# The MLP's last block: two pairs of K tiles as seven products in its first down pair and one in its second, rows turned by GpSimd's queue

## The chip, the cores and the metric

The kernel runs on one core of a Trainium2 chip. The metric is the device time of one execution in microseconds (us), as the median of several runs. A core has five engines with a queue of instructions each: TensorE (PE, matrix products into the accumulators in PSUM), VectorE (DVE, elementwise work and 32x32 transposes), ScalarE (ACT, elementwise work and functions), GpSimd (POOL, here mostly an issuer of DMAs) and SyncE (SP, here only an issuer of DMAs). Each engine runs its own queue strictly in order, and waits for the others by semaphores. So an instruction that waits also holds up everything behind it in its queue.

## The reference

The reference is a decoder trunk of two layers on 256 positions of width 2048: layer 0 with dilated attention, layer 1 with a sparse attention. Behind its attention each layer has an MLP and a gated embedding ("ple"):

```python
hn = rmsnorm(h, mlp_norm_g[i])
h = h + jnp.square(jax.nn.relu(hn @ mlp_w1[i])) @ mlp_w2[i]
gate = jax.nn.sigmoid(rmsnorm(h, ple_norm_g[i]) @ ple_w_gate[i])
h = h + (p[i] @ ple_w_proj[i]) * gate
```

All arrays are float32. `mlp_w1[i]` is 2048 x 8192 and `mlp_w2[i]` 8192 x 2048. The change touches only the second product of the MLP, in both layers, and the way its result gets back into the residual stream `h`.

## The kernel before

**Precision.** A float32 product is computed as three products of rounded parts (`terms`, line 464): each operand is split into a high part (type fp32r) and the rest. For weights, ACT makes `whi` from the loaded tile `raw` (line 249), DVE makes `wlo` as the difference (line 257). A weight chunk is a tile of 128 x 1024: two K tiles of 128 rows by 512 columns.

**The MLP.** It is cut into four blocks `b` of 2048 hidden features (`NFB` is 4), each with four quarters `q` of 512 columns. For every block the first product ("up") makes the hidden quarters, which are turned so that features lie on the partitions (`hid[b]`), and the second product ("down") makes four rows of sums, `q` = 0 to 3, each 128 x 2 x 512: 256 tokens by 512 columns. The rows of blocks 0 to 2 are added up in DRAM (`y[q]`, line 849). The last block, `b` = 3, adds what is in `y[q]`, turns the row (`turned`, line 695: a transpose in blocks by DVE into a tile `z`, one DMA out to DRAM, four DMAs back into a tile `w`), adds it to the residual stream (`add_turned`, line 718) and begins the next norm (`in_pairs`, line 725: ACT makes high part and square of four feature tiles, DVE their low parts and the sum of squares `acc`).

**Pairs and seven products.** `pair_major` (line 467) computes two quarters at once, with four accumulator banks for them. An item of its order is either one chunk of one quarter (`q0` or `q1`: two K tiles, two halves of tokens, three terms: 12 matmuls), or a pair of K tiles for both quarters by seven block products in place of eight (Strassen's scheme in Winograd's form). Such a seven-product pair is four items, in the text called a, b, t and u, with 6, 3, 6 and 6 matmuls. The items a and b use loaded chunks, t and u use sums of these that DVE makes (`make_t`, line 537; `make_u`, lines 542 and 543). The forms of the hidden features that it multiplies (`hf`, lines 782 to 794) are made once in `up`. Four of its products go to banks of their own, which `seven_sums` (line 805) adds up behind the last seven-product pair.

**The last block.** Before the change the first down pair of the last block (`down_mixed(3, 0)`, rows 0 and 1) has one seven-product pair, K tile pair 1, in the order (0,0) (0,2) (0,3), a b t u, (1,0) (1,2) (1,3), then chunks 4 to 7 of both rows. Rows 2 and 3 are not made as a pair: `downs(3, 2)` and `downs(3, 3)` run plainly, one after the other, eight chunks of 12 matmuls each (`token_major`, line 575). Their evacuation, line 857, adds the accumulator to the sums so far, which two DMAs (`fetch`, line 843) have brought from `y[2]` and `y[3]`. Rows 0 and 1 are added to `y[q]` by an accumulating DMA into the row (line 897). All four rows of the last block are turned by SP's queue, the same that loads the weights. Rows 0, 2 and 3 use the tiles `z` and `w`, of which there is one each; row 1 uses two tiles of the ring of rows (`second`).

**What sets the order.** `Program.run` (line 127) goes through the items. At item n it issues, in this order: the loads up to item n + 7 as far as one of five buffers is free, the high part of item n + 4 with its sum by DVE (`make_t`, `make_u`) if it has one, the low part of item n + 3, then one step of every evacuation under way (each `yield` in the code is the end of one step), and then the matmuls of item n. Evacuations are thus counted in items, not in time: `turned` issues its transpose at one item, the DMA out at the next, the DMAs in two items later, and the row is added two items after that.

**Behind the MLP.** `ple` has two projections (`w_proj`, two items) that need only the embedding, then 16 items of two gate quarters, interleaved two and two by `taken_late` (line 650). Their chunk c reads the feature tiles 2c and 2c + 1, so row 2 is wanted from the ninth gate item on and row 3 from the thirteenth. Behind the ninth, `norm.factor` (line 322) puts two small matmuls on PE that read `acc`, the sum of squares over all 16 feature tiles.

Of the kernel before, what the change touches and what calls it, by code (L numbers as in the profile page):

```python
# [11 lines left out]
F32R = mybir.dt.float32r  # L12
# [3 lines left out]
P = 128  # L16
# [18 lines left out]
DMA_AHEAD = 7  # L35
SPLIT_AHEAD = 3
RAW_BUFS, HI_BUFS, LO_BUFS = 5, 6, 5
MIXED_DOWN = 1
MIXED = (2, 3, 5, 6)
REST = ((6, 8, 2, 3), (4, 4, 2, 3))  # L40

# [3 lines left out]
def mixed(b, q):  # L45

    return MIXED[:4 if b else 3]


def f32(ap):  # L50
    return ap.bitcast(F32)
# [116 lines left out]
def kernel(ctx: ExitStack, tc: tile.TileContext, a: dict, out: bass.AP):  # L168
# [549 lines left out]
    def add_turned(q, w):  # L718

        for n in range(2):  # L720
            xn = xp[2 * q + n].rearrange("p (f a r) -> p f a r", a=4, r=32)
            wn = w.rearrange("p a (f r) -> p f a r", r=32)[:, 4 * n:4 * n + 4]
            nc.vector.tensor_add(xn, wn, xn)

    def in_pairs(make, q):

        for n in (0, 2):
            gs = [make(4 * q + n + i) for i in range(2)]
            for g in gs:
                next(g)  # L730
            yield
            for g in gs:
                next(g, None)

    def mlp(layer, xg, norm, to, norm2, opening):
# [15 lines left out]
        def row():  # L751
            return row_tile()
# [9 lines left out]
        def up(b, q, t, late=0):  # L762
            rest = REST[b > 0][q]

            nc.scalar.activation(t, t, AF.Square)
            for _ in range(2 + late):
                yield
            w = yield from turned(t, second if b == 0 and q == 1 else other if q % 2 else new, nc.gpsimd)
            for _ in range(rest):
                yield  # L770
            w4 = w.rearrange("p a (i j r) -> p a (i j) r", j=2, r=32)
            h = cur["z"].tile([P, 2, 4, T], F32R, tag="h", name="h", bufs=4)
            h5 = h.rearrange("p c i (j a r) -> p c a (i j) r", j=2, r=32)
            nc.scalar.copy(h5[:, 0], w4)
            yield
            nc.vector.tensor_sub(h5[:, 1], w4, f32(h5[:, 0]))  # L776
            for i in range(4):
                hid[b][4 * q + i] = (h[:, 0, i], h[:, 1, i])
            if q != MIXED_DOWN // 2:
                return  # L780

            n = MIXED_DOWN % 2 * 4
            a11, a21, a12, a22 = (w4[:, :, n + i] for i in range(4))
            nc.vector.tensor_sub(a22, a21, a22)
            nc.vector.tensor_sub(a21, a11, a21)
            nc.vector.tensor_sub(a11, a11, a22)
            nc.vector.tensor_sub(a12, a12, a11)
            yield
            f = cur["z"].tile([P, 2, 2 * T], F32R, tag="hf", name="hf", bufs=1)
            f5 = f.rearrange("p c (i a r) -> p c a i r", i=4, r=32)  # L790
            nc.scalar.copy(f5[:, 0], w4[:, :, n:n + 4])
            yield
            nc.vector.tensor_sub(f5[:, 1], w4[:, :, n:n + 4], f32(f5[:, 0]))
            turned_forms[b][MIXED_DOWN] = f

        def up_plain(b, q, ps0, ps1, mm):

# [49 lines left out]
        def keep_sum(b, q, t):  # L847

            nc.gpsimd.dma_start(y[q], flat(t), **({"accum_op": ALU.add} if b else {}))

        def down(b, q, ps0, ps1, mm):
            t = row() if b < NFB - 1 else sums_so_far[q]
            for j, ps in enumerate((ps0, ps1)):
                if b < NFB - 1:
                    nc.scalar.copy(t[:, j], ps)
                else:
                    nc.vector.tensor_add(t[:, j], ps, t[:, j])
            yield
            if b < NFB - 1:
                keep_sum(b, q, t)  # L860
                return
            w = yield from turned(t, second if q == 1 else new)
            add_turned(q, w)
            yield
            yield from in_pairs(normed, q)

        def chunks(w, b, q):
            return lambda c: a[w][layer * 128 + (b * 4 + q) * 8 + c]

        def ups(b, q, hooks=None):  # L870
            token_major(chunks("w1", b, q), xg, lambda *ps: up_plain(b, q, *ps), hooks, whole=True)

        def downs(b, q):
            token_major(chunks("w2", b, q), hid[b], lambda *ps: down(b, q, *ps), whole=True)

        def all_forms(these):
            for c in these:
# [4 lines left out]
        def down_mixed(b, q):  # L882
            ts = []

            def sums(aux):
                yield from seven_sums(aux, ts)

            def done(i, ps):
                while not ts:
                    yield  # L890
                t = ts[i]
                nc.vector.tensor_add(t, ps, t)
                yield
                if b < NFB - 1:
                    keep_sum(b, q + i, t)
                    return
                nc.gpsimd.dma_start(flat(t), y[q + i], accum_op=ALU.add)
                for _ in range(3):
                    yield
                w = yield from turned(t, second if q + i == 1 else new)  # L900
                add_turned(q + i, w)
                yield
                yield from in_pairs(normed, q + i)

            m = MIXED_DOWN
            p = [c for c in range(KT // 2) if c != m]
            order = [(0, c) for c in p[:3]]
            order += [(m,)] + [(1, c) for c in p[:3]] if b else [(1, c) for c in p[:3]] + [(m,)]
            for n in (3, 5):
                order += [(i, c) for i in range(2) for c in p[n:n + 2]]  # L910
            pair_major(lambda i, c: a["w2"][layer * 128 + (b * 4 + q + i) * 8 + c], order, hid[b], turned_forms[b],
                       sums, done, {13: [lambda: all_forms(MIXED[3:])]} if (b, q) == (0, 0) else None, (3, 1, 0, 2))

        up_mixed(0, 2)
        for b in range(NFB):
            down_mixed(b, 0)
            if b < NFB - 1:
                up_mixed(b + 1, 0)
                down_mixed(b, 2)
                up_mixed(b + 1, 2)  # L920
        prog.op(lambda: fetch(2))
        prog.op(lambda: fetch(3))
        downs(NFB - 1, 2)
        downs(NFB - 1, 3)
        prog.op(lambda: close_pool("z"))
        prog.op(lambda: open_pool("j"))
        prog.op(lambda: open_pool("R", side="right"))
# [971 lines left out]
def _layout(i):  # L1899
    a = dict(_tables())  # L1900
    a["xT"] = _feature_major(i["x"][0])
    a["xTA"] = _feature_major(i["x"][0][_order()])
    a["pT"] = np.stack([_feature_major(i["p"][l, 0]) for l in range(2)])
    gains = [i["attn_norm_g"][0], i["attn_norm_g"][1], i["mlp_norm_g"][0], i["mlp_norm_g"][1],
             i["ple_norm_g"][0], i["ple_norm_g"][1], i["kv_norm_g"], i["final_norm_g"]]
    a["gains"] = np.stack([g.reshape(KT, P).T for g in gains], 1)
    a["xg0"] = np.concatenate([a["xTA"][:, :2 * T], a["gains"][:, G_ATTN]], 1)
    w = i["a_w_in"][0].reshape(D, 3, NGA, HA, DH)
    a["w_qk"] = _singles(w[:, :2].transpose(0, 3, 1, 2, 4).reshape(D, -1))
    v = w[:, 2]  # L1910
    a["w_v"] = _quads(np.concatenate([t.reshape(D, -1) for h in (0, 4) for t in
                                      (v[:, 0, h:h + 4], v[:, 1:, h:h + 4].transpose(0, 2, 1, 3))], 1))
    a["w_oA"] = _quads(i["a_w_out"][0])
    a["w1"] = np.concatenate([_mixed(_quads(i["mlp_w1"][l]), range(2, 16, 2), mixed) for l in range(2)])
    a["w2"] = np.concatenate([_mixed(np.concatenate([_quads(i["mlp_w2"][l, b * D:(b + 1) * D]) for b in range(NFB)]),
                                     range(0, 14, 2), lambda b, q: (MIXED_DOWN,)) for l in range(2)])
    a["w_gate"] = np.concatenate([_quads(i["ple_w_gate"][l]) for l in range(2)])
    a["g_last"] = np.broadcast_to(i["final_norm_g"][D - 512:], (P, 512))
    a["w_proj"] = np.concatenate([_quads(i["ple_w_proj"][l]) for l in range(2)])
    a["w_kv"] = _quads(i["w_kv_shared"])  # L1920
    qg = i["b_w_qg"][0]
    a["w_q"] = _singles(qg[:, :HB * DH])
    gate = np.concatenate([qg[:, HB * DH:], np.zeros((D, 64 - 3 * HB), np.float32)], 1)
    a["w_g"] = gate.reshape(KT, P, 64).transpose(1, 0, 2).reshape(P, CH)
    a["w_oB"] = _quads(i["b_w_out"][0])
    a["w_c1"] = np.concatenate([i[n].reshape(8, 4, P, 256).transpose(0, 2, 1, 3).reshape(8, P, CH)
                                for n in ("cmp_w1_k", "cmp_w1_v")])
    for n in ("k", "v"):
        a["w2_" + n] = i["cmp_w2_" + n].reshape(2, P, DH).transpose(1, 0, 2)
        a["pe_" + n] = i["cmp_pe_" + n].T  # L1930
    return {n: np.ascontiguousarray(v) for n, v in a.items()}
# [20 lines left out]
```

## Time and profile before

| what | us |
|---|---|
| median of 3 runs (2421.16 to 2421.32) | 2421.16 |
| the profiled execution, its own time | 2421.02 |
| its span, first to last instruction | 2419.1 |
| PE busy, L499 (all pairs) and L595 (all plain quarters) among it | 2409.0 |
| DVE busy | 1988.5 |
| ACT busy | 1420.2 |
| the last block's first down pair in layer 1, from 2221.75 | 42.84 |
| its two plain quarters, from 2264.59 to 2308.11 | 43.52 |

The busy times are sums over the whole span. The granted clock of TensorE was 0.999. Line numbers in the profile are those of the code above. An operation is told as out<-in: `wlo<-raw,whi` is a low part, `ts<-raw` the sum t, `raw<-ts,raw` and `raw<-raw` the sum u, `z<-y` the transpose of a row, `dU<-z` and `w<-dU` the DMAs of its turn, `x<-w,x` its addition to the residual stream. In a timeline the columns are start, busy time, engine, line, operation, count, and in brackets the idle time before with what ended it. Instructions on one engine overlap a little, so that the next start is what one costs, not its busy time.

### The profile page before, as it was taken

The page shows a single profiled execution, that of the slowest core. Times are in us where ns is not written, and L with a number is a line of the kernel's source. Part 1 is how long each engine was busy: PE and PEld are TensorE (multiplying, and loading weights), DVE is VectorE, ACT ScalarE, POOL GpSimd, SP SyncE. Part 2 cuts the span into 40 slices and gives each one's busy share as a digit, 9 for nine tenths or more (in the row PEclk, how much of TensorE's full clock was granted, in tenths as well). Part 3 has the DMA queues.
Part 4 walks back from the last instruction along what each step waited for, and adds up shares of the span by engine and source line. Part 5 has one row for each costly group of instructions (what it writes and reads, how often), then busy time and mean ns, then how long its engine had stood idle before and what let it go on. Part 6 is the DMA issues. An engine that isn't in the chain of part 4 may idle for free.

```text
span 2419.1 us, 33339 instructions
## 1 busy us (share of the span) xinstructions
PE 2409.0 (100%) x11643; PEld 2029.3 (84%) x11643; DVE 1988.5 (82%) x2944; ACT 1420.2 (59%) x2069; POOL 122.0 (5%) x214
## 2 busy tenths in 40 slices
PE   9999999999999999999999999999999999999998
PEld 8888888888888888888888889988888888888887
DVE  7867687688898898896777989867899898889776
ACT  6544444566555655564564788756655565556456
POOL 0000000000001000100000000000100100100000
PEclk9999999999999999999999999999999999999999
DMA  8667666777778777879786854477867877777974
GB/s 284 200 220 213 199 206 196 220 222 247 231 244 242 255 211 241 244 253 283 251 245 204 262 173 121 129 235 210 251 231 234 246 254 220 242 252 224 297 240 148
DMA packets 167271, 549.05 MB, mean 227 GB/s; under 512 B 20096, under 2 KB 35904, under 8 KB 167104
## 3 DMA queue, kind: packets, MB, share of 16 engines
q1 hardware_dynamic: 150672, 494.73, 63.7%
q0 software_dynamic: 15856, 51.41, 8.5%
q8 instruction: 91, 1.49, 0.3%
q10 hardware_dynamic: 576, 0.79, 0.1%
q14 instruction: 76, 0.62, 0.1%
HBM read 500.20 MB, written 46.66 MB: 226 GB/s over the span
## 4 chain that ended last, share of the span: by engine, by line
PE 98%; DMA 1%; DVE 0%; ACT 0%; issue 0%; ACTq 0%; DVEq 0%
PE at L499 40%; PE at L595 14%; PE mm L595 13%; PE mm L390 11%; PE mm L499 7%; PE mm L392 6%; PE at L390 1%; DMA raw<-in_w 1%; PE at L392 1%; PE at L1774 1%; PE mm L1798 0%; PE mm L1537 0%; PE mm L1538 0%; PE mm L1004 0%; PE mm L1006 0%; PE mm L1005 0%
## 5 line engine op out<-in xcount | busy, mean ns | idle before, releaser
L257 DVE TENSOR_TENSOR wlo<-raw,whi 128x1024 fp32r<-128x1024 f32 (+1 forms) x943 | 1090.6, 1176 | 247.3 <-ACT whi L249 63.9
L249 ACT CAST whi<-raw 128x1024 fp32r<-128x1024 f32 (+1 forms) x943 | 932.8, 1017 | 471.9 <-PE mm L595 101.8
L499 PE MATMUL at<-whi,h 128*128 128x512 f32 x1624 | 500.6, 389 | 0.4 <-DVE h L776 0.4
L390 PE MATMUL mm<-xa,whi 128*128 128x512 f32 x1104 | 372.4, 396 | 0.0
L499 PEld LDWEIGHTS at<-whi,h 128*128 128x128 f32 x1624 | 304.9, 188 | 64.6 <-DVE h L776 1.3
L499 PE MATMUL at<-whi,xa 128*128 128x512 f32 x1144 | 352.3, 389 | 0.0
L499 PE MATMUL at<-wlo,h 128*128 128x512 f32 x812 | 315.9, 389 | 0.0
L392 PE MATMUL mm<-xa,wlo 128*128 128x256 f32 x1104 | 274.2, 278 | 0.0
L499 PEld LDWEIGHTS at<-whi,xa 128*128 128x128 f32 x1144 | 214.7, 188 | 44.6
L499 PE MATMUL at<-wlo,xa 128*128 128x512 f32 x572 | 222.5, 389 | 0.0
L392 PEld LDWEIGHTS mm<-xa,wlo 128*128 128x128 f32 x1104 | 207.4, 188 | 17.6
L390 PEld LDWEIGHTS mm<-xa,whi 128*128 128x128 f32 x1104 | 193.5, 188 | 31.0 <-issue 0.4
L595 PE MATMUL at<-whi,xa 128*128 128x512 f32 x672 | 208.4, 392 | 0.0
L595 PE MATMUL mm<-whi,xa 128*128 128x512 f32 x656 | 202.7, 390 | 0.0
L499 PEld LDWEIGHTS at<-wlo,h 128*128 128x128 f32 x812 | 152.4, 188 | 31.5
L249 ACT CAST whi<-ts 128x1024 fp32r<-128x1024 f32 x68 | 71.5, 1051 | 156.8 <-DVE ts L537 106.9
L595 PEld LDWEIGHTS at<-whi,xa 128*128 128x128 f32 x672 | 125.2, 189 | 26.0 <-issue 0.6
L595 PEld LDWEIGHTS mm<-whi,xa 128*128 128x128 f32 x656 | 122.5, 188 | 25.0
L595 PE MATMUL at<-wlo,xa 128*128 128x512 f32 x336 | 130.8, 390 | 0.0
L595 PE MATMUL mm<-wlo,xa 128*128 128x512 f32 x328 | 127.7, 389 | 0.0
L499 PEld LDWEIGHTS at<-wlo,xa 128*128 128x128 f32 x572 | 107.4, 188 | 22.3
L499 PE MATMUL mm<-whi,xf 128*128 128x512 f32 x324 | 99.8, 389 | 0.0
(433 smaller groups left out, 3222.2 us busy)
## 6 DMA issues: line engine op xcount, KB each, us to landing
raw<-in_w SPq DMA_DIRECT2D x512, 512.0 KB, 4.8
raw<-in_w_qk SPq DMA_DIRECT2D x96, 512.0 KB, 4.1
raw<-in_w_gate SPq DMA_DIRECT2D x64, 512.0 KB, 4.5
raw<-in_w_kv SPq DMA_DIRECT2D x48, 512.0 KB, 4.4
raw<-in_w_v SPq DMA_DIRECT2D x47, 512.0 KB, 4.5
y<-y POOLq DMA_DIRECT2D x32, 512.0 KB, 5.5
raw<-in_w_q SPq DMA_DIRECT2D x32, 512.0 KB, 4.2
raw<-in_w_oB SPq DMA_DIRECT2D x32, 512.0 KB, 4.2
```

Source lines behind the costliest of these rows:

```text
L249: nc.scalar.copy(hi[:, c], t[:, c])
L257: nc.vector.tensor_sub(lo[:, c], t[:, c], f32(hi)[:, c])
L390: nc.tensor.matmul(ps, hi[:, col:col + P], rhs, start=first, stop=False)
L392: nc.tensor.matmul(ps[:, :T], lo[:, col:col + P], rhs[:, :T], start=False, stop=last)
L499: nc.tensor.matmul(ps, x_, w_, start=b not in touched, stop=end and last[b] == n and i == 2)
L595: nc.tensor.matmul(st[j], *parts[j][i], start=k == i == 0, stop=k == kt - 1 and i == 2)
L1774: nc.tensor.transpose(tr[:, i * P:(i + 1) * P], src, ident)
```

## The change

Three things change, in both layers.

- The first down pair of the last block takes K tile pairs 1 and 0 as seven products, in the order (0,2) (0,3), pair 1, (1,2) (1,3), pair 0, and then chunks 4 to 7 as before.
- Rows 2 and 3 are made by `down_mixed(3, 2)` in place of the two plain quarters, with K tile pair 1 as seven products and the order of the other blocks. What `y[2]` and `y[3]` hold is fetched behind items 10 and 11 of it, and added by one more DVE addition.
- All four rows of the last block are turned in the tiles `z` and `w` (row 1 no longer in tiles of its own), and by GpSimd's queue instead of SP's.

The forms of K tile pair 0 are made in `up` as well, for the last block alone, and there are two buffers of `hf` in place of one. The layout of the weights in DRAM follows.

```diff
-MIXED_DOWN = 1
+def mixed_down(b, q):
+    return (1, 0) if (b, q) == (NFB - 1, 0) else (1,)
...
-            if q != MIXED_DOWN // 2:
+            if q:
                 return
-
-            n = MIXED_DOWN % 2 * 4
-            a11, a21, a12, a22 = (w4[:, :, n + i] for i in range(4))
-            nc.vector.tensor_sub(a22, a21, a22)
-            nc.vector.tensor_sub(a21, a11, a21)
-            nc.vector.tensor_sub(a11, a11, a22)
-            nc.vector.tensor_sub(a12, a12, a11)
-            yield
-            f = cur["z"].tile([P, 2, 2 * T], F32R, tag="hf", name="hf", bufs=1)
...
+            fs = {}
+            for c in sorted(set(mixed_down(b, 0) + mixed_down(b, 2))):
+                a11, a21, a12, a22 = (w4[:, :, 4 * c + i] for i in range(4))
+                nc.vector.tensor_sub(a22, a21, a22)
+                nc.vector.tensor_sub(a21, a11, a21)
+                nc.vector.tensor_sub(a11, a11, a22)
+                nc.vector.tensor_sub(a12, a12, a11)
+                fs[c] = cur["z"].tile([P, 2, 2 * T], F32R, tag="hf", name="hf", bufs=2)
+            f5 = {c: f.rearrange("p c (i a r) -> p c a i r", i=4, r=32) for c, f in fs.items()}
+            yield
+            for c in fs:
+                nc.scalar.copy(f5[c][:, 0], w4[:, :, 4 * c:4 * c + 4])
+            yield
+            for c in fs:
+                nc.vector.tensor_sub(f5[c][:, 1], w4[:, :, 4 * c:4 * c + 4], f32(f5[c][:, 0]))
+                turned_forms[b][c] = fs[c]
...
                 t = ts[i]
                 nc.vector.tensor_add(t, ps, t)
+                if (b, q) == (NFB - 1, 2):
+                    nc.vector.tensor_add(t, t, sums_so_far[q + i])
                 yield
                 if b < NFB - 1:
                     keep_sum(b, q + i, t)
                     return
-                nc.gpsimd.dma_start(flat(t), y[q + i], accum_op=ALU.add)
-                for _ in range(3):
-                    yield
-                w = yield from turned(t, second if q + i == 1 else new)
+                if q == 0:
+                    nc.gpsimd.dma_start(flat(t), y[q + i], accum_op=ALU.add)
+                    for _ in range(3):
+                        yield
+                w = yield from turned(t, new, nc.gpsimd)
                 add_turned(q + i, w)
                 yield
                 yield from in_pairs(normed, q + i)
 
-            m = MIXED_DOWN
-            p = [c for c in range(KT // 2) if c != m]
-            order = [(0, c) for c in p[:3]]
-            order += [(m,)] + [(1, c) for c in p[:3]] if b else [(1, c) for c in p[:3]] + [(m,)]
-            for n in (3, 5):
-                order += [(i, c) for i in range(2) for c in p[n:n + 2]]
-            pair_major(lambda i, c: a["w2"][layer * 128 + (b * 4 + q + i) * 8 + c], order, hid[b], turned_forms[b],
-                       sums, done, {13: [lambda: all_forms(MIXED[3:])]} if (b, q) == (0, 0) else None, (3, 1, 0, 2))
+            m = mixed_down(b, q)
+            p = [c for c in range(KT // 2) if c not in m]
+            if len(m) == 2:
+                order = [(0, p[0]), (0, p[1]), (m[0],), (1, p[0]), (1, p[1]), (m[1],)]
+            elif b:
+                order = [(0, c) for c in p[:3]] + [(m[0],)] + [(1, c) for c in p[:3]]
+            else:
+                order = [(i, c) for i in range(2) for c in p[:3]] + [(m[0],)]
+            for n in (4, 6):
+                order += [(i, c) for i in range(2) for c in (n, n + 1)]
+            pair_major(lambda i, c: a["w2"][layer * 128 + (b * 4 + q + i) * 8 + c], order, hid[b], turned_forms[b], sums, done,
+                       {(0, 0): {13: [lambda: all_forms(MIXED[3:])]},
+                        (NFB - 1, 2): {10: [lambda: fetch(2)], 11: [lambda: fetch(3)]}}.get((b, q)), (3, 1, 0, 2))
 
         up_mixed(0, 2)
         for b in range(NFB):
             down_mixed(b, 0)
             if b < NFB - 1:
                 up_mixed(b + 1, 0)
-                down_mixed(b, 2)
+            down_mixed(b, 2)
+            if b < NFB - 1:
                 up_mixed(b + 1, 2)
-        prog.op(lambda: fetch(2))
-        prog.op(lambda: fetch(3))
-        downs(NFB - 1, 2)
-        downs(NFB - 1, 3)
```

The functions `down` and `downs` (lines 851 to 865, 873 and 874) go, and the layout of `w2` is told the new pairs (lines 1915 and 1916).

More of the change, by code (lines that the diff above doesn't have):

```diff
@@ L778, in up @@
                 hid[b][4 * q + i] = (h[:, 0, i], h[:, 1, i])
-            if q != MIXED_DOWN // 2:
+            if q:
                 return
-            n = MIXED_DOWN % 2 * 4
-            a11, a21, a12, a22 = (w4[:, :, n + i] for i in range(4))
-            nc.vector.tensor_sub(a22, a21, a22)
-            nc.vector.tensor_sub(a21, a11, a21)
-            nc.vector.tensor_sub(a11, a11, a22)
-            nc.vector.tensor_sub(a12, a12, a11)
+            fs = {}
[7 more added lines that the diff above has]
+            f5 = {c: f.rearrange("p c (i a r) -> p c a i r", i=4, r=32) for c, f in fs.items()}
             yield
-            f = cur["z"].tile([P, 2, 2 * T], F32R, tag="hf", name="hf", bufs=1)
-            f5 = f.rearrange("p c (i a r) -> p c a i r", i=4, r=32)
-            nc.scalar.copy(f5[:, 0], w4[:, :, n:n + 4])
+            for c in fs:
+                nc.scalar.copy(f5[c][:, 0], w4[:, :, 4 * c:4 * c + 4])
             yield
-            nc.vector.tensor_sub(f5[:, 1], w4[:, :, n:n + 4], f32(f5[:, 0]))
-            turned_forms[b][MIXED_DOWN] = f
+            for c in fs:
+                nc.vector.tensor_sub(f5[c][:, 1], w4[:, :, 4 * c:4 * c + 4], f32(f5[c][:, 0]))
+                turned_forms[b][c] = fs[c]
         def up_plain(b, q, ps0, ps1, mm):
@@ L849, in keep_sum @@
             nc.gpsimd.dma_start(y[q], flat(t), **({"accum_op": ALU.add} if b else {}))
[L851 to L857, printed above, removed]
-            yield
[L859 to L863, printed above, removed]
-            yield
-            yield from in_pairs(normed, q)
         def chunks(w, b, q):
@@ L871, in ups @@
             token_major(chunks("w1", b, q), xg, lambda *ps: up_plain(b, q, *ps), hooks, whole=True)
-        def downs(b, q):
-            token_major(chunks("w2", b, q), hid[b], lambda *ps: down(b, q, *ps), whole=True)
         def all_forms(these):
@@ L896, in done @@
                     return
-                nc.gpsimd.dma_start(flat(t), y[q + i], accum_op=ALU.add)
-                for _ in range(3):
-                    yield
-                w = yield from turned(t, second if q + i == 1 else new)
+                if q == 0:
[3 more added lines that the diff above has]
+                w = yield from turned(t, new, nc.gpsimd)
                 add_turned(q + i, w)
@@ L1915, in _layout @@
     a["w2"] = np.concatenate([_mixed(np.concatenate([_quads(i["mlp_w2"][l, b * D:(b + 1) * D]) for b in range(NFB)]),
-                                     range(0, 14, 2), lambda b, q: (MIXED_DOWN,)) for l in range(2)])
+                                     range(0, 16, 2), mixed_down) for l in range(2)])
     a["w_gate"] = np.concatenate([_quads(i["ple_w_gate"][l]) for l in range(2)])
```

## The prediction

> **What bounds the kernel.** I read the page's first part, then the waits of PE alone, then the chain in order of time:
>
> ```profile
> PE 2409.0 (100%) x11643; PEld 2029.3 (84%) x11643; DVE 1988.5 (82%) x2944; ACT 1420.2 (59%) x2069; POOL 122.0 (5%) x214
> PE at L499 <- DVE h L776: 0.4, 2, 0.3
> 2286.52 21.76 PE at L595 x96
> ```
>
> PE has work all the time, and over the whole kernel it waits 0.4 us for the hidden features and hardly for anything else. The last row gives the price of a matmul: 21.76 / 96 = 0.2267 us. So each matmul taken out saves that, and each microsecond for which PE is made to wait is lost in full. The question is whether the other engines keep up. The windows of layer 1, over the first down pair, the two plain quarters and the start of ple (length, then busy time and count by engine PE, PEld, DVE, ACT, POOL, clock, DMA share, GB/s):
>
> ```profile
> 2221.20:2264.10 42.90, 42.90 (x191) 35.55 (x190) 34.32 (x33) 24.09 (x26) 7.56 (x13) 1.00 0.78 251
> 2264.10:2307.90 43.80, 43.80 (x195) 36.25 (x195) 32.30 (x42) 22.73 (x35) 0.89 (x1) 1.00 0.98 303
> 2307.90:2335.30 27.40, 27.40 (x122) 22.71 (x121) 21.99 (x33) 17.80 (x30) 0.00 (x0) 1.00 0.79 241
> ```
>
> DVE is busy for three quarters of each, and the DMA engines for 98% of the second.
>
> **What goes.** A seven-product pair is 21 matmuls, two plain chunks 24. Each layer gets one more in the first pair and one in rows 2 and 3: 6 matmuls fewer, 1.36 us, 2.72 us in both layers. That is 0.11% of the time, and the most that there is to gain.
>
> **What DVE gets.** A stretch in which DVE never rests gives the cost by the distance of the starts:
>
> ```profile
> 2201.95 1.22 DVE L537 TENSOR_TENSOR ts<-raw 128x1024 f32<-128x1024 f32 x1
> 2203.08 0.69 DVE L257 TENSOR_TENSOR wlo<-raw,whi 128x512 fp32r<-128x512 f32 x1
> 2203.68 0.68 DVE L542 TENSOR_TENSOR raw<-ts,raw 128x512 f32<-128x512 f32 x1
> 2204.40 0.69 DVE L543 TENSOR_TENSOR raw<-raw 128x512 f32<-128x512 f32 x1
> 2205.01 1.22 DVE L257 TENSOR_TENSOR wlo<-ts,whi 128x1024 fp32r<-128x1024 f32 x1
> ...
> 2232.25 4.59 DVE L257 TENSOR_TENSOR wlo<-raw,whi 128x1024 fp32r<-128x1024 f32 x4
> 2236.76 1.22 DVE L776 TENSOR_TENSOR h<-w,h 128x1024 fp32r<-128x1024 f32 x1
> ```
>
> The sum t costs 1.13, half a low part 0.60, the sum u 0.72 + 0.61 = 1.33, a low part 4.51 / 4 = 1.13; I take 1.13 for every other operation of this size. A seven-product pair costs DVE 3 x 1.13 + 0.60 + 1.13 + 1.33 = 6.45 us for 21 x 0.2267 = 4.76 us of PE; two plain chunks 2.26 for 5.44. The seven-product pairs live on items made ahead.
>
> **The first down pair** (rows of DVE, ACT, and PE's first product of it):
>
> ```profile
> 2221.75 0.61 PE L499 MATMUL at<-whi,h 128*128 128x512 f32 x2
> 2223.05 1.18 DVE L257 TENSOR_TENSOR wlo<-raw,whi 128x1024 fp32r<-128x1024 f32 x1
> 2224.16 1.21 DVE L826 TENSOR_TENSOR y<-at,y 128x1024 f32<-128x1024 f32 x1
> 2225.40 1.34 ACT L828 ACTIVATE y<-y,col 128x512 f32<-128x512 f32 x2 [3.22 <-DVE y L826]
> 2227.74 1.04 ACT L249 CAST whi<-ts 128x1024 fp32r<-128x1024 f32 x1
> 2231.09 1.24 DVE L706 STREAM_TRANSPOSE z<-y 128x1024 f32<-128x1024 f32 x1
> ```
>
> PE starts the pair at 2221.75. The second seven-product pair's u begins after 84 matmuls, and its third matmul, the first that reads the low part, after 86: 2241.25. DVE is free at 2223.05 and has until then, in this order: t; half a low part; L826; u; low parts of t and u; two low parts; row 3's transpose (1.16, from 2231.09 to 2232.25); low part of a; t; half a low part; u; low part of t; row 2's h; low part of u. That is 11 x 1.13, 2 x 0.60, 2 x 1.33 and 1.16: 17.45. To it comes a wait of 1.08 at the first u: its high part stands behind ACT's relu and square of row 3, which wait for L826. The distance 2225.40 to 2227.74, put behind an L826 that now begins at 2224.78, brings this high part to 2229.4, where DVE would have come at 2228.4. The last low part is ready at 2241.67, with 0.09 us of overlap: PE waits **0.42 us** per layer. Nearest bounds: nothing, if DVE gains half a microsecond anywhere, and 1.
>
> The forms of K tile pair 0 (four small subtractions, a copy, a low part) fall into block 2's second down pair; the small ones are under 0.3 us each. I cost them at nothing: DVE rests there, and each PE item is 2.72 us. Without that cover they would cost up to 2 us per layer.
>
> **Rows 0 and 1, in the second down pair.** Rows of before: POOL's turn of rows in up with ACT's next use, which waits for the landing; row 1's addition, its accumulating DMA and its transpose; the seven sums; the next norm.
>
> ```profile
> 2223.43 0.56 POOL L203 DMA_DIRECT2D dU<-z  x1 [39.89 <-DVE z L706]
> 2228.87 2.23 POOL L207 DMA_DIRECT2D w<-dU  x4 [4.88 <-ACT whi L249]
> 2235.62 1.05 ACT L774 CAST h<-w 128x1024 fp32r<-128x1024 f32 x1 [2.09 <-DMA w<-dU]
> 2232.62 0.56 POOL L203 DMA_DIRECT2D dU<-z  x1 [1.52 <-DVE z L706]
> 2238.11 2.18 POOL L207 DMA_DIRECT2D y<-dU  x4 [4.92 <-DMA dU<-z]
> 2247.61 1.05 ACT L774 CAST h<-y 128x1024 fp32r<-128x1024 f32 x1 [0.91 <-DMA y<-dU]
> ...
> 2239.03 0.68 DVE L809 TENSOR_TENSOR y<-mm,y 128x512 f32<-128x512 f32 x1
> 2241.68 3.49 DVE L257 TENSOR_TENSOR wlo<-raw,whi 128x1024 fp32r<-128x1024 f32 x3
> ...
> 2264.79 1.23 DVE L892 TENSOR_TENSOR y<-at,y 128x1024 f32<-128x1024 f32 x1 [1.44 <-PE at L499]
> 2266.32 0.89 POOL L897 DMA_DIRECT2D y<-y  x1 [3.17 <-DVE y L892]
> 2276.95 1.25 DVE L706 STREAM_TRANSPOSE y<-y 128x1024 f32<-128x1024 f32 x1 [2.71 <-DMA y<-y]
> 2295.11 0.47 DVE L360 SCALAR_TENSOR_TENSOR xa<-x,gains,xa 128x256 fp32r<-128x256 f32 x1
> 2295.50 0.41 DVE L286 TENSOR_TENSOR acc<-acc,sq 128x256 f32<-128x256 f32 x1
> 2295.84 0.47 DVE L360 SCALAR_TENSOR_TENSOR xa<-x,gains,xa 128x256 fp32r<-128x256 f32 x1
> ```
>
> From the end of a transpose (2231.09 + 1.24) to its DMA out: 0.3 us; from a DMA out to the DMAs in: 5.44 and 5.49. From these to the landing: 6.75 or 9.50. The seven sums take 2.65; a half of the next norm (two feature tiles) 2 x 0.73 = 1.46. Now with P the start of the second pair. Row 1's transpose waits twice: for its accumulating DMA, which before landed 10.6 after its issue (2266.32 to 2276.95), some P + 12.4, and, new, for `z`, which row 0 holds until its DMA out has landed. DVE is through row 1's addition at P + 1.4; t, half a low part, u, a low part and row 0's transpose, 5.35 in all, bring it to P + 6.8; + 0.3 + 5.4 is P + 12.5. So the new wait takes the place of one as long, and its cost is nothing. But behind it stand, where DVE before had room, the low parts of 8, 9 and 10. Then row 0's addition waits for the landing at 12.5 + 6.75 = P + 19.3, and goes on till 20.5; low part, seven sums, low part, half a norm bring DVE to P + 26.9. Row 1's DMAs in can't start before row 0 has left `w` (20.6): landing P + 27.3, addition till 28.5, item 13's low part at 29.6. PE reads it after 131 matmuls, at P + 29.7. It is just in time, and from here DVE rests no more: three halves of a norm, seven low parts (14 to 20), row 2's accumulator, its sums so far and its transpose are 3 x 1.46 + 9 x 1.13 + 1.16 = 15.7. Row 2 is transposed at P + 45.3, which is 2.5 us behind the end T of the pair (P + 189 x 0.2267 = P + 42.8). Row 2's last product stands 24 matmuls ahead of T, 5.4 us; with DVE free, the four operations behind it, 4.6 us, would be done before T.
>
> **Rows 2 and 3, in ple.** Row 3's chain before, and PE's first reading of the sum of squares:
>
> ```profile
> 2308.11 0.61 PE L595 MATMUL mm<-whi,pg 128*128 128x512 f32 x2
> 2327.11 1.29 DVE L723 TENSOR_TENSOR x<-w,x 128x512 f32<-128x512 f32 x2 [3.92 <-DMA w<-dU]
> 2328.32 2.36 DVE L257 TENSOR_TENSOR wlo<-raw,whi 128x1024 fp32r<-128x1024 f32 x2
> 2334.32 0.42 DVE L286 TENSOR_TENSOR acc<-acc,sq 128x256 f32<-128x256 f32 x1
> 2338.03 0.50 PE L295 MATMUL mm<-ones,acc 128*128 128x1 f32 x4
> ```
>
> Before, `acc` was done at 2334.7 and read at 2338.03, T + 29.92: 3.3 us to spare. Now row 2's DMA out leaves at T + 2.8, the DMAs in at T + 8.2, landing T + 15.0, addition till T + 16.2. Row 3 has to wait for `w`: in from T + 16.3, landing T + 23.05. Then its addition (1.21), three low parts and three halves of a norm, row 2's second among them: 8.98, `acc` at T + 32.0. PE waits **2.1 us** per layer. If PE already waited at item 13, T is later by as much, and the two aren't to be added.
>
> The Trainium skill, "DMA: Bandwidth & Descriptors", section "Anatomy of one DMA — SWDGE (gpsimd) path", gives a GpSimd DMA 2.0 us and its bytes at 436 GB/s, an estimate of 3.2 us for a row out and 2.3 for a quarter of it in. By that the turns would be some 5 us shorter each, no wait would be left, and the sum would be rival A's. The traced 5.44 and 6.75 speak against it.
>
> **Sum.** 2 x (-1.36 + 0.42 + 2.1) = +2.3 us on the profiled execution's own 2421.02 (its span of 2419.1 and 1.9 around it; 0.14 below the median): **2423.3**. From landings no trace of before shows, the bounds are: 5.54 us instead of 6.75 (row below) takes 1.2 off each of four landings in a row, and no wait in ple is left; 9.50 for one of them, as row 3's above, adds 2.75 to the layer.
>
> ```profile
> 1069.30 2.23 POOL L207 DMA_DIRECT2D w<-dU  x4 [4.48 <-DMA dU<-z]
> ...
> 1074.84 1.05 ACT L774 CAST h<-w 128x1024 fp32r<-128x1024 f32 x1 [0.47 <-DMA w<-dU]
> ```
>
> **The rivals.**
> - A, the gain is kept: DMAs land in 5.5 us, `acc` is in time. SP's queue, rid of the turns, speaks for it, and 5.54 above. Time: 2421.02 - 2.72 + 0 to 0.84, about 2418.7. Chance 0.25.
> - B, slower: rows 1 and 3, each kept from `w` until its forerunner is added, land late. Speaking for it: the 9.50 above and 98% of DMA share just there; against it: rows 2 and 3 now leave that stretch. Place: row 3's landing, ahead of `acc`; price 2.75 per layer, 5.5 on the forecast: 2428.8. It decides from 1.3 us more wait per layer. Chance 0.25.
> - C, the first pair chokes: ACT stands at row 3's h for its landing, and high parts behind it come late. By the order above it is ready at 2250.4, wanted at 2253.5, so 3 us to spare; a miss by 3 more would cost 6 in all: some 2427. Chance 0.05.
> - The forecast, most of the 2.72 or somewhat more given back: 2420.7 to 2426. Chance 0.45.
>
> **How the numbers follow.** 2423.3; the range 2418.5 to 2429 takes in A and B's price, and leaves the worst of B and C out. About 0.2% (4.8 us) is what a measurement can tell from no change. Faster by that would need more than all 12 matmuls: 0.01. Slower: B and half of C's spread, 0.26. Within: 0.73.
>
> **What would show it.** PE's matmuls fewer by 12; waits of PE for DVE's `acc` (L286) at L295 in both layers, near 2 us each, and for `wlo` in the first pair, under 1. Row 2's transpose 2 to 3 us behind the last product of the pair. Right means also that `dU<-z` to `w<-dU` stays near 5.4 on POOL. I am wrong if PE waits nowhere (A), if it waits at item 13 for `wlo` behind row 1's landing, or if a place that I cost at nothing shows a wait: the forms in block 2, or the loads `raw`, which seven-product pairs hold longer.

## The result, and the profile after

| kernel | median of 4 runs, us | lowest to highest | profiled execution | its span |
|---|---|---|---|---|
| before | 2421.16 | 2421.11 to 2421.32 | 2421.02 | 2419.1 |
| after | 2449.52 | 2447.91 to 2450.45 | 2449.26 | 2447.5 |

The ratio is 1.0116, with an interval of 1.0099 to 1.0134. The forecast was 2423.3, its range ended at 2429.0, so the time lies some 20 us outside it. The sign of rival B was right, its size was not.

The first part of the page of after, and the waits of PE (line, what it waited for, total, times, longest). The lines of after named here are 3 higher than those of before: 252 is `whi`, 260 `wlo`, 289 the addition to `acc`, 298 the small matmuls on it, 502 the pairs, 598 the plain products, 709 the transpose, 726 the addition of a row. 814 to 817 are the seven sums, 878 is the addition of the accumulator.

```profile
PE 2418.6 (99%) x11631; PEld 2032.9 (83%) x11631; DVE 2018.1 (82%) x2982; ACT 1430.1 (58%) x2081; POOL 144.4 (6%) x254
```

```profile
PE at L502 <- DVE wlo L260: 7.9, 2, 4.0
PE mm L298 <- DVE acc L289: 6.6, 2, 4.1
PE mm L598 <- DVE wlo L260: 3.1, 2, 2.8
...
PE mm L502 <- DVE wlo L260: 0.7, 2, 0.4
PE at L598 <- ACT whi L252: 0.5, 2, 0.4
PE at L598 <- DVE wlo L260: 0.5, 1, 0.5
```

Two things are to be seen. The waits add up to 19.3 us, where before had 0.4 (a wait of 1.1 for a constant, which both have, is left out). And PE is busy for 9.6 us *more* than before, with 12 matmuls fewer: 2.72 us fewer at 0.2267 each, so the matmuls that are left took 12.3 us longer. The account is 18.9 of waits + 12.3 of slower matmuls - 2.7 of matmuls left out = 28.5; the spans differ by 28.4.

**Where PE waits.** The second down pair in layer 1 starts at P = 2279.13. Parts of its timeline on DVE, on POOL and on PE (start, busy time, engine, line, operation, count, and in brackets the idle time before and what ended it):

```profile
2279.33 1.23 DVE L878 TENSOR_TENSOR y<-at,y 128x1024 f32<-128x1024 f32 x1 [1.44 <-PE at L502]
...
2292.14 1.25 DVE L709 STREAM_TRANSPOSE z<-y 128x1024 f32<-128x1024 f32 x1 [3.37 <-DMA dU<-z]
...
2298.49 1.30 DVE L726 TENSOR_TENSOR x<-w,x 128x512 f32<-128x512 f32 x2 [1.72 <-DMA w<-dU]
...
2310.53 1.29 DVE L726 TENSOR_TENSOR x<-w,x 128x512 f32<-128x512 f32 x2 [4.70 <-DMA w<-dU]
2311.74 1.22 DVE L260 TENSOR_TENSOR wlo<-raw,whi 128x1024 fp32r<-128x1024 f32 x1
```

```profile
2286.21 0.56 POOL L206 DMA_DIRECT2D dU<-z  x1 [3.17 <-DVE z L709]
2292.31 2.24 POOL L210 DMA_DIRECT2D w<-dU  x4 [5.54 <-DMA dU<-z]
2294.54 0.57 POOL L206 DMA_DIRECT2D dU<-z  x1
2302.10 2.20 POOL L210 DMA_DIRECT2D w<-dU  x4 [7.00 <-DVE y L814]
```

```profile
2308.37 0.61 PE L502 MATMUL at<-whi,h 128*128 128x512 f32 x2
2313.01 0.80 PE L502 MATMUL at<-wlo,h 128*128 128x512 f32 x1 [4.03 <-DVE wlo L260]
2313.61 1.05 PE L502 MATMUL at<-whi,h 128*128 128x512 f32 x2
2319.36 0.63 PE L502 MATMUL at<-whi,h 128*128 128x512 f32 x2
```

Read from the end: PE waits 4.03 us for a low part. That low part stands on DVE directly behind the addition of row 1, and this one waited 4.70 us for the landing of row 1 (`w<-dU`). Nothing is slow on DVE; it stands, in order, in front of a DMA. POOL's row at 2302.10 names the sum of L814 as what ended its wait; that sum writes no tile of the turn and only ended in the same moment, while row 1's DMA out (2294.54) had landed after 6.9 us, at 2301.4. This is item 13, the place that the prediction had "just in time". The same is seen in layer 0 (3.87 us of the 7.9).

**The price of a wait is more than the wait.** The windows of PE around it (length, busy time and count of PE, PEld, DVE, ACT, POOL, then granted clock, DMA share, GB/s):

```profile
2305.00:2308.00 3.00, 3.00 (x15) 2.49 (x14) 0.83 (x3) 0.37 (x1) 0.40 (x1) 1.00 0.84 227
2309.00:2312.00 3.00, 0.00 (x0) 0.00 (x0) 1.47 (x3) 0.75 (x3) 0.00 (x0) 0.96 0.80 310
2312.00:2318.00 6.00, 4.99 (x12) 3.93 (x13) 6.00 (x11) 4.61 (x10) 0.00 (x0) 0.50 0.52 156
2319.00:2325.00 6.00, 6.00 (x28) 4.96 (x27) 6.00 (x7) 3.05 (x4) 0.00 (x0) 1.00 0.74 238
```

PE's granted clock is 0.50 in the window behind the wait, and 12 matmuls take 4.99 us there, where 28 take 6.00 afterwards. A pair of them shows 1.05 in place of 0.63 in the timeline above. So a wait of 4 us is followed by some 5 us of work at half speed, which is 2.5 us lost again. The Trainium skill, "TensorE: Matmul & The Clock Gate", section "Part 1: The HAM clock gate (the "warmup" mystery)", says that TensorE falls to half its clock after an idle window of about 3.4 us and needs about 3.4 us of work to come back. The trace agrees in kind. In size: the clock stood at 0.50 from 2311.8 to 2318.6, which is twice 3.41 us, and for 3.41 us each time in layer 0; and it fell when PE had stood for 2.8 us.

In ple, row 3 does the same to `acc`: DVE's addition of row 3 waits for its landing, and PE waits for `acc`.

```profile
2354.52 1.29 DVE L726 TENSOR_TENSOR x<-w,x 128x512 f32<-128x512 f32 x2 [6.93 <-DMA w<-dU]
...
2363.19 0.42 DVE L289 TENSOR_TENSOR acc<-acc,sq 128x256 f32<-128x256 f32 x1
```

```profile
2363.66 1.01 PE L298 MATMUL mm<-ones,acc 128*128 128x1 f32 x4 [4.10 <-DVE acc L289]
```

### The profile page after: what moved, and what is told of

Its sections match the earlier page's. It is cut to its first block, busy times and chain, and to the rows that moved or that the text cites. A ratio compares the mean times of both kernels' runs of the same rounds, so it can differ in the third digit from the quotient of the medians.

```text
span 2447.5 us, 33396 instructions
## 1 busy us (share of the span) xinstructions
PE 2418.6 (99%) x11631; PEld 2032.9 (83%) x11631; DVE 2018.1 (82%) x2982; ACT 1430.1 (58%) x2081; POOL 144.4 (6%) x254
## 5 line engine op out<-in xcount | busy, mean ns | idle before, releaser
L502 PE MATMUL at<-whi,h 128*128 128x512 f32 x1832 | 567.5, 391 | 0.1
L502 PEld LDWEIGHTS at<-whi,h 128*128 128x128 f32 x1832 | 346.0, 189 | 73.1 <-DVE h L779 1.0
L502 PE MATMUL at<-wlo,h 128*128 128x512 f32 x916 | 358.5, 391 | 7.9 <-DVE wlo L260 7.9
L395 PEld LDWEIGHTS mm<-xa,wlo 128*128 128x128 f32 x1104 | 207.4, 188 | 17.6
L502 PEld LDWEIGHTS at<-wlo,h 128*128 128x128 f32 x916 | 172.9, 189 | 44.7 <-DVE wlo L260 8.7
```

What stands on the lines that cost most here:

```text
L395: nc.tensor.matmul(ps[:, :T], lo[:, col:col + P], rhs[:, :T], start=False, stop=last)
L502: nc.tensor.matmul(ps, x_, w_, start=b not in touched, stop=end and last[b] == n and i == 2)
```

## The experiments

Three explanations were open, and they ask for different cures. *Queue*: the turn by GpSimd's queue makes the rows land late. *Sharing*: the rows are late since row 1 now waits for `z` and `w` (row 3 did so before too). *Products*: the seven-product pairs themselves ask too much of DVE or of the loads. Beside these stood the question whether a wait costs more than its length. Each experiment below is timed beside the kernel before on the same chip; its median was 2421.55 beside the last four and 2421.24 beside the others.

### One part undone

**Row turns by SP's queue again**, on after, with the shared tiles kept:

```diff
-                w = yield from turned(t, new, nc.gpsimd)
+                w = yield from turned(t, new)
```

> The changed kernel with its four turns on SP's queue again (shared z and w kept). Theory Q (the late landings are the price of GpSimd's queue: in the changed kernel a DMA out took 6.1 to 7.6 us there and the DMAs in 6.2 to 8.8, and VectorE stands in order behind the landing of rows 1 and 3): the waits at item 13 and at the sum of squares shrink from 4 us to under 2 each, too short for the clock to fall, 2420 to 2428 us. Theory S (rows 1 and 3 are held up by sharing z and w with their forerunners): the waits stay, 2442 to 2452.

2426.41, ratio 1.0023 (1.0013 to 1.0032): 23 of the 28 us are gone by the queue alone. What is left are single waits of 2.3 us and 1.7 us. In layer 1 row 1 is added without any wait.

**Rows 1 and 3 in tiles of their own**, on after, with GpSimd's queue kept (before, only row 1 had them):

```diff
-                w = yield from turned(t, new, nc.gpsimd)
+                w = yield from turned(t, second if i else new, nc.gpsimd)
```

> The changed kernel with tiles of their own for rows 1 and 3, still on GpSimd's queue. Theory Q: row 1's DMA out still stands in the queue behind row 0's DMAs in, so it lands as late: 2444 to 2452 us. Theory S: the waits go, 2419 to 2426.

2456.09, ratio 1.0145 (1.0128 to 1.0162). It isn't faster than after, so sharing is not what costs. It shows why: with a tile of its own, row 1 is transposed 3 us earlier (9.9 us behind the start of the pair, in after 13.0), but its DMA out still leaves right behind row 0's four DMAs in (15.6 behind it, in after 15.4), and its DMAs in come later still, since they wait for that DMA, which takes longer (`y` is the row's own tile here):

```profile
2296.86 0.57 POOL L206 DMA_DIRECT2D dU<-y  x1
2308.27 2.20 POOL L210 DMA_DIRECT2D y<-dU  x4 [10.84 <-DMA dU<-y]
```

**The turn alone**, on before: the plain quarters and the one seven-product pair stay, all rows are turned in `z` and `w` by GpSimd's queue (the change is at both calls of `turned` in the last block):

```diff
-            w = yield from turned(t, second if q == 1 else new)
+            w = yield from turned(t, new, nc.gpsimd)
...
-                w = yield from turned(t, second if q + i == 1 else new)
+                w = yield from turned(t, new, nc.gpsimd)
```

> The kernel before with nothing but the new turn (shared z and w, GpSimd's queue), no product changed. If the loss needs the seven-product pairs too (they fill VectorE and shorten the items in which a row's DMAs may land): within 2 us of before, 2420 to 2424, PE waiting under 1 us in each layer. If the new turn alone is the loss: 2435 to 2450.

2438.85, ratio 1.0071 (1.0056 to 1.0086), without one matmul less. So the turn by itself loses 17.6 us, where the whole change loses 28.4. Its waits:

```profile
PE mm L595 <- DVE wlo L257: 4.2, 2, 3.0
PE mm L295 <- DVE acc L286: 3.7, 2, 2.6
PE at L595 <- DVE wlo L257: 2.4, 3, 1.4
```

**The products alone**: after with SP's queue *and* tiles of their own for rows 1 and 3, so that the matmuls and their order are what is changed (row 3's own tiles aside):

```diff
-                w = yield from turned(t, new, nc.gpsimd)
+                w = yield from turned(t, second if i else new)
```

> The products of the change alone: SP's queue, and tiles of their own for rows 1 and 3. If the products alone leave too little room for the rows: waits as in e1_sp, 2423 to 2430 us. If the turn is all of the loss: 2418.5 to 2420.5.

2423.59, ratio 1.0012 (1.0002 to 1.0021). The 2.72 us of matmuls left out don't show: its waits add up to 4.7, none over 1.5. *Products* is worth a few us against the gain, not the loss. The turn alone (17.6) and the products alone (2.4) add up to 20.0; the other 8 us appear only when both are there. By SP's queue, tiles of their own are 2.8 us faster than shared ones (2423.59 against 2426.41), but the two intervals overlap.

**The first down pair's second seven-product pair alone**, on before (rows 2 and 3 plain, turns as before; the forms in `up` as in the change):

```diff
-MIXED_DOWN = 1
+def mixed_down(b, q):
+    return (1, 0) if (b, q) == (NFB - 1, 0) else (1,)
...
             if b < NFB - 1:
                 up_mixed(b + 1, 0)
                 down_mixed(b, 2)
```

> The first down pair's second seven-product pair alone; rows 2 and 3 plain, all turns as before the change. By the prediction's walk 3 matmuls fewer (0.68 us) and a wait of 0.42 at u per layer: 2420.6, from 2420 to 2421.5. If the denser first pair delays rows 0 and 1 further: over 2422.

2421.0, ratio 1.0 (0.999 to 1.0009). At u of the second seven-product pair PE waits 0.3 us, in one layer alone, where 0.42 in each were predicted. This part of the prediction held in its place and its order of size; the 0.5 us that it would gain can't be told from nothing here.

### The landing taken out of DVE's way

An addition that comes later in the order leaves DVE free until its row has landed. First rows 1 and 3 both three items later, with the sum of squares read two items later:

```diff
                 w = yield from turned(t, new, nc.gpsimd)
+                for _ in range(3 * i):
+                    yield
...
-            hooks = {4: [lambda: norm.factor(rows=not last)]} if q == 0 else \
+            hooks = {6: [lambda: norm.factor(rows=not last)]} if q == 0 else \
```

> The changed kernel with two edits that remove no work: rows 1 and 3 are added to the residual stream three items later, so that VectorE does not stand in order before a landing, and the root of the norm behind ple's projections is taken two chunks later (hook 6 in place of 4). If the loss is VectorE's standing in order, and the clock that falls after each such wait: the waits at item 13 and at the sum of squares go, the clock stays at 1.00, 2418.5 to 2421 us. If it is too much work for VectorE, or too much for the DMA engines: waits for the low parts stay, and more than 2430.

2424.34, ratio 1.0014 (1.0004 to 1.0023): GpSimd's queue and the shared tiles are unchanged, row 1 in layer 1 lands only 1.2 us earlier (30.1 behind the start of the pair, in after 31.3) and row 3 no earlier, and 25 of the 28 us are gone. It is 3 us above what was expected. What is left is one wait of 1.8 us for `acc`, at another norm, 1.1 for `h`, and short ones. Behind the 1.8 us the clock was 0.50 from 2401.4 to 2404.8, with 9 matmuls in 3.30 us, some 1.7 us lost again.

**Row 1 alone** three items later:

```diff
+                for _ in range(0 if q else 3 * i):
+                    yield
```

> The changed kernel with one of the two edits of e5_late: row 1 alone is added three items later. The wait of 4 us at item 13 in each layer should go, and with it its fall of the clock; the wait at the sum of squares stays, since rows 2 and 3 are untouched. If waits and their clock are each worth about half of the loss: 2432 to 2440 us. If the wait at item 13 only moves on to the sum of squares (VectorE behind all the same): over 2444.

2438.67, ratio 1.0072 (1.0057 to 1.0087), 10.9 below after. The 7.9 us of item 13 are gone, and PE's busy time falls by 5.0, from 2418.6 to 2413.6. The waits in ple stay: 6.9 for `acc`, and those for low parts grow from 3.6 to 5.6. So somewhat less than half of the loss, 10.9 of 28.4, goes with row 1's addition, the rest with rows 2 and 3.

**Row 1 later, rows 2 and 3 by SP's queue:**

```diff
-                w = yield from turned(t, new, nc.gpsimd)
+                w = yield from turned(t, new, nc.sync if q else nc.gpsimd)
+                for _ in range(0 if q else 3 * i):
+                    yield
```

> e5a_row1 with rows 2 and 3 turned by SP's queue, in the same shared tiles. In e1_sp a turn on SP took about 3 us less from transpose to landing than on GpSimd's queue, and the spare of the sum of squares needs some 4: waits of 0 to 2 us per layer at the sum of squares, too short for the clock, 2419 to 2424 us. If the queue is not what makes rows 2 and 3 late: as e5a_row1.

2423.47, ratio 1.0005 (0.9996 to 1.0014). PE is busy for 2407.4, 1.1 us above 2409.0 - 2.72, and the clock is 0.999 over the span, as before. No wait is over 1.0, the 1.1 for a constant aside.

### The price of a wait on PE

To measure it by itself, DVE gets useless work in the kernel before, 5 or 8 additions of a full row ahead of row 3's last two feature tiles, so that `acc` comes late in ple. Nothing else is changed:

```diff
-            yield from in_pairs(normed, q)
+            pairs = in_pairs(normed, q)
+            for step in range(3):
+                if q == 3 and step == 2:
+                    for _ in range(5):
+                        nc.vector.tensor_add(t, t, t)
+                if next(pairs, True):
+                    break
+                yield
```

> The kernel before with five additions of a dead row to itself (1.13 us each, 5.7 in all) on VectorE ahead of row 3's last two feature tiles in both layers, so that the sum of squares, which has 3.0 to 3.3 us to spare, is late by some 2.4. Theory C (PE's clock falls to half only after it stood some 3 us): the price is the wait itself, 2 x 2.4: 2426 us, clock 1.00 behind it. If any wait costs clock: 2430 or more.

> The same with eight additions (9.0 us): a wait of some 5.8 per layer. Theory C: the clock falls in the wait and stays at half for some 5 us of work, 2.5 to 3 us more per layer: 2 x 5.8 + 5 to 6, 2437 to 2439 us. If the wait alone is paid: 2432.8.

The medians are 2430.32 (ratio 1.0038, 1.0024 to 1.0051) and 2440.3 (1.008, 1.0067 to 1.0094). With 5 additions the two layers came out unequal, which makes one run answer the question. Its timeline of PE:

```profile
1183.10 1.01 PE L295 MATMUL mm<-ones,acc 128*128 128x1 f32 x4 [3.84 <-DVE acc L286]
...
2345.94 0.61 PE L295 MATMUL mm<-ones,acc 128*128 128x1 f32 x4 [0.86 <-DVE acc L286]
```

And its windows of 40 us from 20 us ahead of each to 20 behind:

```profile
1163.00:1203.00 40.00, 36.16 (x151) 29.56 (x150) 26.77 (x34) 18.50 (x25) 0.00 (x0) 0.91 0.65 199
2323.00:2363.00 40.00, 39.14 (x175) 32.14 (x174) 29.49 (x38) 20.51 (x27) 0.00 (x0) 1.00 0.69 220
```

Behind 0.86 us the clock is 1.00 and nothing but the wait is lost. Behind 3.84 us it is 0.91 on average, and PE is busy for 2411.4 in the whole kernel, 2.4 more than before, for the same matmuls. With 8 additions both waits are long (5.0 and 5.82, 10.8 together), and PE is busy for 2413.7, 4.7 more: 2.4 for each fall, on average. "The wait alone" would have given 2421.55 + 10.8 = 2432.4; with the falls it is 2437.1. The execution in the profile took 2438.19, the median is 2440.3; what the others lost more is not in this trace. The waits were sized wrongly in the expectation of the first (2.4 each).

The runs together show where it decides. In all traces here waits up to 1.53 us were followed by the full clock. The kernel with all turns by SP's queue shows two longer ones, one of each kind, on PE's timeline and in the windows behind:

```profile
1138.60 0.50 PE L502 MATMUL at<-wlo,h 128*128 128x512 f32 x1 [2.33 <-DVE wlo L260]
...
1183.66 0.61 PE L298 MATMUL mm<-ones,acc 128*128 128x1 f32 x4 [1.71 <-DVE acc L289]
```

```profile
1139.00:1145.00 6.00, 6.00 (x28) 4.96 (x27) 6.00 (x13) 5.57 (x9) 0.00 (x0) 1.00 0.64 184
...
1185.00:1188.00 3.00, 3.00 (x8) 2.32 (x8) 2.08 (x3) 0.20 (x1) 0.00 (x0) 0.50 0.69 208
```

2.33 us left the clock at 1.00, 1.71 us, with four products of one column behind it, brought it to 0.50. Nor is a longer wait always followed by a fall. In the version with tiles of their own for rows 1 and 3 a wait of 3.28 us was not (nor was one of 2.41 us there, and one of 2.52 us in the version with row 1 alone later):

```profile
2363.58 0.50 PE L598 MATMUL mm<-wlo,xa 128*128 128x512 f32 x1 [3.28 <-DVE wlo L260]
```

```profile
2363.00:2366.00 3.00, 2.42 (x10) 1.80 (x10) 3.00 (x6) 1.75 (x5) 0.00 (x0) 1.00 0.40 126
```

What decides is where the wait falls. In each trace the clock changes only at instants that lie whole multiples of 3.41 us apart; in after they are 1141.0, 1144.4, 1185.4, 1188.8, 1192.2, 1195.6, 2311.8, 2318.6, 2363.0 and 2369.8. Cut every trace here into stretches of 3.41 us at these instants, and add up how long PE stood in each. At full clock, every stretch with 2.02 us or more was followed by half the clock, and every one with 1.85 us or less by full clock, except three of 1.70 to 1.82 us that held the four products of one column as well. The 3.28 us fell across an edge, 1.75 us on one side and 1.54 on the other; 2.33, 2.41 and 2.52 us were divided too.

After has five waits of 2.5 us and more, all followed by half the clock: 3.87, 2.83 and 2.51 in layer 0, 4.03 and 4.10 in layer 1. The clock stood at 0.50 for 3.41 us behind each of the first three and for 6.83 us, part of the wait among it, at the others; PE worked at half speed for 21.9 us of it. Half of that, 11.0 us, is lost, and the slower matmuls were 12.3. The same page and section of the Trainium skill call the window in which activity is watched free-running; a grid that does not move with the waits agrees with that. But no idle window of 3.4 us was needed here: 2.02 us of idle time in a stretch of 3.41 were enough.

### With the long waits gone

The version with row 1 later and rows 2 and 3 by SP, now with the sum of squares read one item later:

```diff
-            hooks = {4: [lambda: norm.factor(rows=not last)]} if q == 0 else \
+            hooks = {5: [lambda: norm.factor(rows=not last)]} if q == 0 else \
```

> e6_mix with the root of the norm behind the projections taken one chunk later (hook 5 in place of 4): its last wait of 1.0 us for the sum of squares goes. 12 matmuls fewer (2.7 us) against the waits left (0.4 at u per layer, 0.8 for a row of hidden features): 2419 to 2420.5 us, within 0.2% of before. If something other than PE's waits eats the gain: 2422 or more.

And the same without the second seven-product pair in the first down pair:

```diff
-    return (1, 0) if (b, q) == (NFB - 1, 0) else (1,)
+    return (1,)
```

> e9_hook5 with one seven-product pair in the first down pair, as before the change; so 6 matmuls fewer than before (1.36 us) and no wait at u: 2419.5 to 2421 us. If the first pair's density costs more than its wait of 0.4 shows: faster than e9_hook5 by over 1 us.

2420.93 (ratio 0.9998, 0.9989 to 1.0007) and 2419.68 (0.9993, 0.9984 to 1.0002), of 11 runs each. The second leaves out only 6 matmuls, 1.36 us. Both intervals hold 1: with every long wait gone, what is left of the gain can't be told from nothing. In the first, short waits of PE, none over 0.5 us, still add up to 2.9 us, where before had 0.4.

## Why the prediction was wrong

**What held.** PE was the bound, and the 12 matmuls went. The first down pair cost what was worked out: 0.42 us per layer were predicted at u of the second seven-product pair, and PE waited 0.40 in layer 1 of after. In the second pair the first half of the chain came close: row 0 landed at P + 19.4 (2298.49) for a predicted P + 19.3, row 1's transpose began at P + 13.0 for P + 12.5. The first of these is luck in part: row 0's leg from DMA out to DMAs in took 6.10 for 5.44, its leg to the landing 6.18 for 6.75. The places were right too: item 13 behind row 1, `acc` behind row 3, in both layers; only the first was held to be just in time. Rows 1 and 3 landed late behind their forerunners, as rival B has it, but not by B's cause, `w` held until the forerunner is added.

**The step that failed first** is the term "Row 1's DMAs in can't start before row 0 has left `w` (20.6): landing P + 27.3". The landing came at P + 31.4 (2310.53):

| leg of row 1 | predicted | after, layer 1 |
|---|---|---|
| DMA out to DMAs in | 5.44 | 7.56 (2294.54 to 2302.10) |
| DMAs in to landing | 6.75 | 8.43 (2302.10 to 2310.53) |
| DMAs in, from P | 20.6 | 23.0 |

The tile `w` was free by 2299.8, when row 0 had been added, 2.3 us ahead of row 1's DMAs in, so its leaving did not bind. Row 1's DMA out left only when row 0's four DMAs in had been issued (2292.31 to 2294.54), as one queue issues both; that is 0.9 us. The rest is that the legs are longer than the rows they were taken from; the prediction itself had named a leg near 5.4 as a sign of being right. Here are the windows of the two rows of before that it read (5.44 and 5.49), and those of legs from DMA out to DMAs in, in after and in the turn alone:

```profile
2223.40:2228.90 5.50, 5.50 (x26) 4.57 (x25) 5.08 (x7) 3.47 (x5) 0.59 (x2) 1.00 0.53 185
2232.60:2238.10 5.50, 5.50 (x26) 4.53 (x25) 5.50 (x6) 3.41 (x4) 0.56 (x1) 1.00 0.91 308
```

```profile
2247.80:2252.70 4.90, 4.90 (x23) 4.04 (x23) 4.87 (x6) 1.68 (x2) 0.58 (x2) 1.00 0.93 350
2286.20:2292.30 6.10, 6.10 (x29) 5.05 (x28) 2.20 (x3) 3.07 (x4) 0.56 (x1) 1.00 0.97 333
2294.50:2302.10 7.60, 7.60 (x35) 6.28 (x35) 5.85 (x7) 2.89 (x7) 0.60 (x2) 1.00 0.89 285
2338.60:2345.70 7.10, 7.10 (x33) 5.85 (x33) 5.32 (x6) 3.48 (x7) 0.52 (x1) 1.00 0.93 280
```

```profile
2278.50:2287.90 9.40, 9.40 (x44) 7.76 (x42) 2.50 (x3) 3.85 (x4) 0.55 (x1) 1.00 1.04 357
...
2328.80:2332.50 3.70, 3.70 (x18) 3.05 (x17) 3.70 (x4) 1.25 (x2) 0.56 (x1) 1.00 0.66 219
```

The row of 5.44 was taken where the DMA engines were busy for 53%. In the stretch to which it was applied (the last three rows of after) they were at 89 to 97%, and the legs took 6.1 to 7.6 us. In the turn alone the same kind of transfer took 9.4 us at 104% and 3.7 us at 66%. The warning was on the prediction's own page: 98% of DMA share in the row of windows that it quoted for the plain quarters. It was used to speak for rival B, and not to size a leg. But the DMA share does not set the leg by itself: the prediction's other row, 5.49, was at 91%, and in after a leg of the row turned in `up` took 4.8 us at 93%. Of the 38 transfers `dU<-z` by GpSimd in after, those below a share of 0.75 (from issue to landing) landed in 2.9 to 5.1 us, those above 0.8 in 4.4 to 6.9, and the eight at 1.00 or more in 4.4 to 6.6. So a busy stretch allows a long leg and does not force it, and no run changed the load alone: why just these legs are long stays open. The Trainium skill's "DMA: Bandwidth & Descriptors", section "Anatomy of one DMA — SWDGE (gpsimd) path", gives 2.0 us and the bytes at 436 GB/s, an estimate of 3.2 us for this transfer; of the windows above only the quiet one comes near it, with 3.7.

**The second step that failed** is "each microsecond for which PE is made to wait is lost in full". It is lost in full, and where PE stands for 2 us or more in one of the stretches of 3.41 us, another 1.7 to 3.1 us with it in after, by the clock. By itself that makes 11.0 of the 12.3 us of slower matmuls, and these are 12.3 of the 28.4. It also explains why B was priced too low: its 2.75 us per layer more in ple, on a wait of 2.1, makes a wait long enough for a fall each.

**The third** is the wait for `acc`: 2.1 us per layer were predicted, and it was 2.51 and 4.10; in layer 0, 2.83 more came shortly ahead of it at a low part in ple. In layer 1 the first product of ple, T, starts at 2328.91. The timeline of DVE and of POOL there:

```profile
2327.61 1.24 DVE L709 STREAM_TRANSPOSE z<-y 128x1024 f32<-128x1024 f32 x1
```

```profile
2329.14 0.54 POOL L206 DMA_DIRECT2D dU<-z  x1 [23.74 <-DVE z L709]
2336.34 2.22 POOL L210 DMA_DIRECT2D w<-dU  x4 [6.66 <-DMA dU<-z]
2338.56 0.57 POOL L206 DMA_DIRECT2D dU<-z  x1
2345.74 2.19 POOL L210 DMA_DIRECT2D w<-dU  x4 [6.62 <-DMA dU<-z]
```

The prediction had row 2's transpose done 2.5 us behind T. It was done at T (2327.61 + 1.24): DVE used the time that PE had lost at item 13, and the delay that was to be carried into ple was gone. Row 2's DMA out left at T + 0.2 instead of T + 2.8. Still row 3 landed at T + 25.6 (2354.52) for a predicted T + 23.05, since its own legs were 7.18 and 8.78 us and its DMA out stood behind row 2's four DMAs in, as row 1's did behind row 0's. So the later wait, too, is the same mis-sized term, and "the two aren't to be added" was wrong: they are two losses.

**What is behind it, in one line.** The turn by GpSimd's queue is the larger part (17.6 alone; undone, 5 us stay), it costs through DVE standing in order (undone by adding rows later, 3 us stay, the queue unchanged), and PE's slower clock adds about two thirds of what the waits cost.

**Open.** Why the queue of SP, in place of GpSimd's, lets DVE pass: in layer 1 row 1 was transposed at P + 9.9 there, as row 0's DMA out let go of `z` 3 us sooner, and added at P + 28.2 without a wait. Not every DMA is faster there: row 1's own DMA out took 9.1 us to land. A DMA share alone does not tell the queues apart: row 2's DMA out landed in 6.9 us at a share of 0.84 by GpSimd in after, and in 4.2 us at 0.89 by SP's queue. But on SP's queue the turn also stands in order with the weight loads, and what that changes was not tried by itself.

## What to carry to other kernels

Where an engine runs in order and an addition waits for a landing, list what stands behind it and who reads that; putting the addition a few items later can be worth more than making the DMA faster. Take a transfer's duration as a range over all rows of its kind in busy stretches, not from the nearest row that has the same code: here one kind of DMA landed in 4.4 to 6.9 us at DMA shares above 0.8. And on the engine that bounds the kernel, count a wait of about 2 us or more at its length plus the clock's price, while several waits of half a microsecond cost only themselves.

## What the runs showed of the hardware

- TensorE's granted clock changed only on a grid of 3.41 us. It fell to 0.50 behind every stretch of the grid in which PE stood for 2.02 us or more, and stayed at 1.00 behind every one with 1.85 us or less, except three of 1.70 to 1.82 us that also held the four products of one column. So a wait of 3.28 us, divided by an edge of the grid, left it at 1.00, and one of 1.71 us brought 0.50. The half clock then lasted 3.41 or 6.83 us.
- The same transfer of 512 KB by GpSimd's queue took 3.7 to 9.4 us from its issue to the issue that waits for it, in one kernel, with the DMA share at 0.66 and 1.04; but in after one took 4.8 us at 0.93 and another 7.2 us at 0.83, so the share alone does not tell it.
